# Sums of gate/up weights by accumulating DMAs, and another order of the seven block products

## The chip, the cores and the metric

The kernel runs on one core of one Trainium2 chip. Its engines are TensorE (PE, with its weight loads as PEld), VectorE (DVE), ScalarE (ACT), GpSimd (POOL) and SyncE (SP), which here issues nearly all transfers. The metric is the time of one execution on the device in microseconds (us), the median of several runs. A profile is one further execution, recorded instruction by instruction.

## The reference, cut to what matters

One decoder layer on 512 tokens of width 1024. Three head groups (mLSTM, SSD, retention) are computed from one input projection; their outputs are concatenated into `mix`. The change lies in what comes after that:

```
x = x + mix @ w_out
h = rmsnorm(x, norm_ffn)                      # y * rsqrt(mean(y*y) + eps) * g
gate, up = jnp.split(h @ w_gate_up, 2, axis=-1)
x = x + (jax.nn.silu(gate) * up) @ w_down
return rmsnorm(x, norm_final)
```

FFN_HIDDEN is 2816. All inputs are float32, and the products keep about that accuracy: each float32 operand is split into a high and a low part (`hi`, `lo`), and a product is three matmuls, hi*hi, hi*lo and lo*hi.

## The kernel before, in words

**Weights.** All weight matrices are packed into one array and cut into chunks, 256 rows by up to 512 columns, held as 128 x 1024 (512 KB). For each chunk `split` (lines 198 to 204) issues a cast on ACT, which makes `hi` (L202), and a subtraction on DVE, which makes `lo` (L203). There are four `hi` and four `lo` buffers. `chunk` (L225) fetches three chunks ahead of the one that the matmuls are about to use.

**Output projection.** `products_f` (L377) multiplies in two passes; the last pass covers two groups of four tiles of 128 features. Where a tile is done, `ev_out` adds it to `x` on DVE (L1125), scales it with the gain of the norm on ACT (L1129, into `y2`), feeds it to the norm and stores it to DRAM (`x2d`, L1131). `Norm.feed` squares a tile (on ACT for even k, L300, on POOL for odd k, L298) and adds the squares in a tree on DVE (L304). `finish` (L307) sums over the features with four tiny matmuls (L310); the result `r2` is needed only where gate and up are scaled.

**Gate and up.** Tokens are cut in two halves, features in two halves, and the columns in six pairs of blocks (five of 512 columns, one of 256: `GU_W`), one block of gate and one of up. In each pair the 2 x 2 block product is done with seven products instead of eight, in the manner of Strassen and Winograd. A product has 24 matmuls (L1164 to L1166) from two chunks. Four quarters of weights come in from DRAM per pair: R11, R12, R22, R21. Four products need sums of quarters: `tb` = R12 + R22, `r12` = R12 + R11, then `r11` = `tb` + R11 and `r21` = `r11` + R21. POOL forms all of them (L911, and L935 and L936 for the next pair), two instructions per sum. Their places in memory are rotated from pair to pair (`nxt`), and a place is loaded anew by SP as soon as its contents are split (`follow`). The other operand, sums of token and feature halves (names S1 to S4), is formed once, by DVE and POOL (L1118), and split by `split_a` (L1112 on ACT, L1113 on DVE). The order of the products is 11, S2, S1, S3, 12, S4, 22; 11 needs only the first half of the features. After each product its result is moved out of the PSUM banks by ACT and DVE (L1195 to L1225).

**Turning.** The results of a pair are transposed on PE in four groups of four (L1176), all 16 of them between the second and the third product of the next pair; the first four tiles go to DRAM (`ad`).

**Down projection.** At the start the residual `x2d` is read back (L1234) and added with transposing matmuls (L1264), then come the products (L1267 to L1269).

**Order of the work.** Each engine runs its instructions in order, and so does SP with its transfers. A scheduler in the framework sets this order when the kernel is built, from the order of the code and its own estimate of durations. Waits are semaphores that an instruction carries.

Of the kernel before, what the change touches and what calls it, by code (L numbers as in the profile page):

```python
# [16 lines left out]
P = 128  # L17
D = 1024
S = 512
NC = 4  # L20
# [99 lines left out]
def trunk(tc, x, xt, wcat, vecs, rows, consts, posn, gfin, out):  # L120
# [6 lines left out]
    with contextlib.ExitStack() as es:  # L127
# [160 lines left out]
        class Norm:  # L288
# [602 lines left out]
        def begin_ffn():  # L891
# [6 lines left out]
            def gload(p, quarter, to):  # L898
                if p < len(GU_W):
                    for s_ in range(2):  # L900
                        bring(GU0 + 8 * p + 2 * quarter + s_, to[s_])

            def pair_jobs(p, U):
                w2 = 2 * GU_W[p]
                nxt = dict(r11=U["spare"], r12=U["r12"], r22=U["tb"], tb=U["r11"], r21=U["r22"], spare=U["r21"])

                def of(r, s_):
# [5 lines left out]
                def sums(s_):  # L913
                    add("tb", "r12", "r22", s_)
                    add("r12", "r12", "r11", s_)

                order = []

                def job(role, s_, before=None, after=None):
                    def run():  # L920
                        if before:
                            before()
# [15 lines left out]
                def tc_():  # L938
                    for i in range(2):
                        add("r11", "tb", "r11", i)  # L940

                def td():
                    for i in range(2):
                        add("r21", "r11", "r21", i)
                    follow(U["r11"])

                def follow(unit, quarter=None, to=None):
# [9 lines left out]
                job("r11", 0, before=(lambda: sums(0)) if p == 0 else None)  # L957

                def after_p1():
                    if p == 0:  # L960
                        sums(1)
                    tc_()
                    if p:
                        follow(U["spare"], R11)

                job("r11", 1, after=after_p1)
                job("r11", 0)
                job("r11", 1)
                job("r12", 0)
                job("r12", 1, after=lambda: follow(U["r12"], R12))  # L970
                job("tb", 0)
                job("tb", 1, after=lambda: follow(U["tb"], R22))
                job("r21", 0)
                job("r21", 1, after=td)
                job("r22", 0)
                job("r22", 1, after=lambda: follow(U["r22"], R21))
                job("r21", 0, after=next_sums)
                job("r21", 1, after=lambda: follow(U["r21"]))
                return order, nxt
# [15 lines left out]
            for q, r in ((R11, "r11"), (R12, "r12"), (R22, "r22")):  # L995
                gload(0, q, roles[r])
# [123 lines left out]
        for last in (False, True):  # L1120
            for gr in range(2):

                def ev_out(t, ps):
                    d = x2[4 * gr + t]
                    dve.tensor_tensor(out=d, in0=ps, in1=d, op=ALU.add)  # L1125
                    if last:
                        k = 4 * gr + t
                        g = vec[:, V_G2 + k:V_G2 + k + 1]
                        act.activation(out=v3(y2[k // 2], 2)[:, k % 2, :], in_=d, func=AF.Copy, scale=g)  # L1129
                        n2.feed(d, t % 2 == 1)  # L1130
# [14 lines left out]
        s3 = [combine(pool, halves(i, 0), halves(i, 1), ALU.subtract) for i in range(2)]  # L1145
        s1 = [combine(dve, halves(i, 1), halves(2 + i, 1), ALU.subtract) for i in range(2)]
        s2 = [combine(dve, s1[i], halves(i, 0), ALU.subtract) for i in range(2)]
        s4 = [combine(pool, halves(2 + i, 0), s2[i], ALU.add) for i in range(2)]
        for name, src in (("S2", s2), ("S1", s1), ("S3", s3), ("12", [halves(2 + i, 0) for i in range(2)]), ("S4", s4), ("22", [halves(2 + i, 1) for i in range(2)])):
            for i in range(2):  # L1150
                split_a(name, i, src[i])
# [17 lines left out]
        def turn(p, w, a):  # L1169


            def go():
                for f in range(w // P):
                    ps = mbank()
                    for c in range(NC):
                        mm(ps[:, c * P:(c + 1) * P], lhsT=a[c][:, f * P:(f + 1) * P], rhs=ident, start=True, stop=True, is_transpose=True)  # L1176
                    kt = 4 * p + f
                    t = slot()
                    act.copy(out=t, in_=ps)
                    if kt < SPILL:  # L1180
                        sp.dma_start(out=ad[kt], in_=t)
                    else:
                        aT[kt] = t
# [3 lines left out]
        def cols(t, w):  # L1187
            return t[:, 0:w]

        for p, w in enumerate(GU_W):  # L1190
            ba = [bank() for _ in range(2)]
            product(ba, "11", w, True)
            s1 = [slot(w=w) for _ in range(2)]
            for c in range(2):
                act.copy(out=s1[c], in_=ba[c][:, 0:w])  # L1195
            if p == 0:
                n2.finish(r2)
            bb = [bank() for _ in range(2)]
            product(bb, "S2", w, True)
            e = [slot(w=w) for _ in range(2)]  # L1200
            for c in range(2):
# [3 lines left out]
            bq = [mbank() for _ in range(2)]  # L1205
            product(bq, "S1", w, True)
            product(bb, "S3", w, False)
# [3 lines left out]
            for c in range(2):  # L1211
                dve.tensor_tensor(out=u[c], in0=bq[c][:, 0:w], in1=u[c], op=ALU.subtract)
            product(ba, "12", w, False)
            g1 = [slot(w=w) for _ in range(2)]
            for c in range(2):
                act.activation(out=g1[c], in_=ba[c][:, 0:w], func=AF.Silu, scale=r2[:, c:c + 1])
            product(bq, "S4", w, False)
# [8 lines left out]
            tail.append(turn(p, w, e + u))  # L1226


        gf = [slot() for _ in range(2)]
        for hf in range(2):  # L1230
            sp.dma_start(out=gf[hf], in_=gfin[512 * hf:512 * hf + 512].partition_broadcast(P))
        for k in range(KD):
            x2[k] = slot()
            sp.dma_start(out=x2[k], in_=x2d[k])  # L1234
# [17 lines left out]
        for n, kc in enumerate(DOWN_ORDER):  # L1252
            w2 = [chunk(), chunk()]
            split_t(n + 2)
            for c in range(NC):
                if n == 0 and c == 2:
                    tail.pop(0)()
# [99 lines left out]
```

## Time and profile before

| | us |
|---|---|
| median of 3 runs (lowest, highest) | 861.02 (860.77, 861.97) |
| the profiled execution | 862.31 |
| its span | 860.5 |
| PE busy | 833.4 (97%) |
| DVE, ACT, POOL busy | 549.5, 375.0, 342.0 |
| bytes moved | 93.41 MB, 109 GB/s over the span |

The span is the time from the first to the last recorded instruction; the profiled execution is 1.8 us longer than it. PE is busy almost throughout, so the question for any change is in which stretches PE stands still or runs at its lower clock, and what it waits for there.

### The profile page before, as it was taken

What the parts mean: (1) busy time and instruction counts of PE and PEld (TensorE: products, weight loads), DVE (VectorE), ACT (ScalarE), POOL (GpSimd) and SP (SyncE); (2) the same over time, 40 slices, a digit from 0 to 9 for tenths busy, and PEclk for the clock granted to TensorE, in tenths of its full rate; (3) what the DMA queues carried; (4) which work ended last, traced back from release to release, by engine and by line L of the source; (5) the groups of instructions that cost most, each with busy time, mean ns of one, the idle gap of its engine ahead of it and who ended that gap; (6) DMA issues with size and microseconds to landing.
All of it is one profiled execution on the core that took longest, in us unless ns stands there. A gap on an engine that the chain in (4) does not pass through costs nothing. (4 is left out here: it accounts for less than half of the span.)

```text
span 860.5 us, 11249 instructions
## 1 busy us (share of the span) xinstructions
PE 833.4 (97%) x4238; PEld 715.4 (83%) x4238; DVE 549.5 (64%) x742; ACT 375.0 (44%) x641; POOL 342.0 (40%) x278
## 2 busy tenths in 40 slices
PE   9999999999999899999999889999999997999997
PEld 9989899898988788888888768787877887888885
DVE  6648677685648978366433989797979787122223
ACT  6344545364534354335312654545353556511113
POOL 2335433242024847613304638283838333920001
PEclk9999999999999999999999979999999999999999
DMA  7423332432234223216321253422232138530002
GB/s 249 153 75 106 98 122 81 126 95 68 98 99 146 71 93 109 74 50 254 138 98 50 98 196 98 146 98 98 99 98 74 50 116 317 204 98 0 1 1 98
DMA packets 32933, 93.41 MB, mean 109 GB/s; under 512 B 3800, under 2 KB 3928, under 8 KB 32880
## 3 DMA queue, kind: packets, MB, share of 16 engines
q1 hardware_dynamic: 32160, 91.58, 32.2%
q10 hardware_dynamic: 720, 1.12, 0.4%
q8 instruction: 33, 0.54, 0.3%
q14 instruction: 20, 0.16, 0.1%
HBM read 87.40 MB, written 5.29 MB: 108 GB/s over the span
## 5 line engine op out<-in xcount | busy, mean ns | idle before, releaser
L203 DVE TENSOR_TENSOR lo<-raw,hi 128x1024 fp32r<-128x1024 f32 (+3 forms) x98 | 131.5, 1346 | 132.9 <-ACT hi L202 132.3
L202 ACT CAST hi<-raw 128x1024 fp32r<-128x1024 f32 (+3 forms) x107 | 104.2, 976 | 161.5 <-PE b L388 79.7
L203 DVE TENSOR_TENSOR lo<-big,hi 128x1024 fp32r<-128x1024 f32 (+1 forms) x79 | 118.2, 1505 | 79.0 <-ACT hi L202 78.3
L202 ACT CAST hi<-big 128x1024 fp32r<-128x1024 f32 (+1 forms) x79 | 77.5, 991 | 135.0 <-PE m L1269 60.6
L387 PE MATMUL b<-s,hi 128*128 128x512 f32 x304 | 120.0, 395 | 0.8 <-ACT s L637 0.8
L388 PE MATMUL b<-s,hi 128*128 128x512 f32 x304 | 119.1, 392 | 0.0
L389 PE MATMUL b<-s,lo 128*128 128x512 f32 x304 | 118.5, 391 | 0.0
L370 PE MATMUL b<-hi,s 128*128 128x384 f32 (+2 forms) x320 | 114.7, 365 | 1.3 <-ACT big L408 1.0
L371 PE MATMUL b<-lo,s 128*128 128x384 f32 (+2 forms) x320 | 115.3, 360 | 0.0
L372 PE MATMUL b<-hi,s 128*128 128x384 f32 (+2 forms) x320 | 113.9, 361 | 0.0
L1165 PE MATMUL b<-lo,s 128*128 128x512 f32 (+1 forms) x240 | 90.3, 377 | 2.6 <-DVE lo L203 2.6
L1164 PE MATMUL b<-hi,s 128*128 128x512 f32 (+1 forms) x240 | 88.7, 376 | 4.0 <-ACT s L1112 3.2
L1166 PE MATMUL b<-hi,s 128*128 128x512 f32 (+1 forms) x240 | 89.7, 376 | 0.0
L387 PEld LDWEIGHTS b<-s,hi 128*128 128x128 f32 x304 | 57.1, 188 | 12.2 <-ACT s L637 1.1
L389 PEld LDWEIGHTS b<-s,lo 128*128 128x128 f32 x304 | 57.1, 188 | 11.5
L388 PEld LDWEIGHTS b<-s,hi 128*128 128x128 f32 x304 | 57.2, 188 | 10.9
L370 PEld LDWEIGHTS b<-hi,s 128*128 128x128 f32 x320 | 60.1, 188 | 6.5 <-ACT big L408 1.2
L371 PEld LDWEIGHTS b<-lo,s 128*128 128x128 f32 x320 | 60.2, 188 | 5.2 <-DVE lo L203 0.4
L372 PEld LDWEIGHTS b<-hi,s 128*128 128x128 f32 x320 | 60.0, 188 | 4.9
L203 POOL TENSOR_TENSOR lo<-raw,hi 128x1024 fp32r<-128x1024 f32 (+1 forms) x9 | 19.5, 2165 | 100.9 <-ACT hi L202 91.3
L618 DVE SCALAR_TENSOR_TENSOR s<-s,vec,s 128x511 f32<-128x511 f32 (+2 forms) x66 | 59.1, 939 | 0.2 <-ACT s L615 0.2
L1164 PEld LDWEIGHTS b<-hi,s 128*128 128x128 f32 x240 | 45.4, 190 | 13.2 <-ACT s L1112 3.6
(296 smaller groups left out, 1612.1 us busy)
## 6 DMA issues: line engine op xcount, KB each, us to landing
raw<-in_wcat SPq DMA_DIRECT2D x67, 512.0 KB, 3.4
big<-in_wcat SPq DMA_DIRECT2D x47, 512.0 KB, 4.5
raw<-in_wcat SPq DMA_DIRECT2D x20, 384.0 KB, 3.1
s<-in_xt SPq DMA_DIRECT2D x16, 256.0 KB, 6.3
s<-mdr SPq DMA_DIRECT2D x12, 256.0 KB, 4.4
s<-adr SPq DMA_DIRECT2D x12, 256.0 KB, 5.9
x2d<-s SPq DMA_DIRECT2D x8, 256.0 KB, 2.0
s<-x2d SPq DMA_DIRECT2D x8, 256.0 KB, 6.8
```

Of the source, the lines that this page charges most:

```text
L202: pin(act.copy(out=hi, in_=raw), first)
L203: pin(eng.tensor_tensor(out=lo, in0=raw, in1=hi.bitcast(F32), op=ALU.subtract), first)
L370: mm(o_, lhsT=hh, rhs=whi[:, k, :], start=kk == 0, stop=False)
L371: mm(o_, lhsT=hh, rhs=wlo[:, k, :], start=False, stop=False)
L372: mm(o_, lhsT=hl, rhs=whi[:, k, :], start=False, stop=kk == KD - 1)
L387: mm(banks[t], lhsT=wh, rhs=rhs_hi[kk], start=a, stop=False)
L388: mm(banks[t], lhsT=wh, rhs=rhs_lo[kk], start=False, stop=False)
L389: mm(banks[t], lhsT=wl, rhs=rhs_hi[kk], start=False, stop=b)
L618: dve.scalar_tensor_tensor(out=a[:, sft:S], in0=u[:, 0:S - sft], scalar=w[3 - sft], in1=a[:, sft:S], op0=ALU.mult, op1=ALU.add)
L1164: mm(o_, lhsT=ah, rhs=whi[:, k, :], start=first and s_ == 0 and k == 0, stop=False, skip_group_check=not first)
L1165: mm(o_, lhsT=ah, rhs=wlo[:, k, :], start=False, stop=False, skip_group_check=not first)
L1166: mm(o_, lhsT=al, rhs=whi[:, k, :], start=False, stop=s_ == 1 and k == 1, skip_group_check=not first)
```

## The change

Four things change in gate/up.

1. Of the four sums of weights in a pair, two are formed by transfers that add to what lies in their destination: `add_chunk` issues them on POOL's queue (`accum_op=ALU.add`). R12 is added onto a place loaded with R22 (`tb`), R11 onto a place loaded with R12 (`r12`). So R11, R12 and R22 are read twice: 14 chunks per pair instead of 8. The other two sums go to DVE (`onto`). POOL adds no weights any more.
2. The products come as 11, S3, S1, S2, 12, S4, 22. S3 needs only the first half of the features, as 11 does, and its operand is now formed and split during the output projection. S3 is copied out by ACT, and S2 accumulates on S3 in the same banks.
3. The squares of the norm overwrite `x` in place (after it is stored), their sums move from DVE to POOL, and the tiny matmuls of `finish` come after S2 in the code (before: after 11).
4. The 16 transposes of a pair are spread over four places, and `x2d` and the final gain are read back during the last pair instead of after it.

```diff
+        def add_chunk(i, t):
+
+            w = len(CHUNKS[i][2])
+            pool.dma_start(
+                out=t[:, 0:2 * w],
+                in_=wcat[offsets[i]:offsets[i] + P * 2 * w].rearrange("(p f) -> p f", p=P),
+                accum_op=ALU.add,
+            )
...
-            def feed(self, x_, on_pool):
+            def feed(self, x_, on_pool, adds=dve, own=True):
                 k, sq = len(self.sq), self.sq
-                sq.append(slot())
+                sq.append(slot() if own else x_)
...
-                    dve.tensor_tensor(out=sq[i], in0=sq[i], in1=sq[j], op=ALU.add)
+                    adds.tensor_tensor(out=sq[i], in0=sq[i], in1=sq[j], op=ALU.add)
...
-                def add(to, x_, y_, s_):
-                    pool.tensor_tensor(out=of(to, s_), in0=of(x_, s_), in1=of(y_, s_), op=ALU.add)
...
+                def onto(to, x_, s_):
+                    dve.tensor_tensor(out=of(to, s_), in0=of(x_, s_), in1=of(to, s_), op=ALU.add)
...
-                def next_sums():
-                    if p + 1 < len(GU_W):
-                        w_ = 2 * GU_W[p + 1]
-                        for i in range(2):
-                            t, a_, b_, c_ = (nxt[r][i][:, 0:w_] for r in ("tb", "r12", "r22", "r11"))
-                            pool.tensor_tensor(out=t, in0=a_, in1=b_, op=ALU.add)
-                            pool.tensor_tensor(out=a_, in0=a_, in1=c_, op=ALU.add)
...
+                def after_11():
+                    if p:
+                        onto("r11", "tb", 1)
+                        follow(U["spare"], R11)
+
+                def after_tb():
+                    if p == 0:
+                        for i in range(2):
+                            onto("r11", "tb", i)
+                    follow(U["tb"], R22)
+
+                def after_21():
+                    for i in range(2):
+                        onto("r21", "r11", i)
+                    follow(U["r11"], R22)
+
+                def after_22():
+                    follow(U["r22"], R21)
+                    gload(p + 1, R12, nxt["tb"], add=True)
...
+                job("r11", 0, (lambda: onto("r11", "tb", 0)) if p else None)
+                job("r11", 1, after_11)
+                job("tb", 0)
+                job("tb", 1, after_tb)
+                job("r12", 0)
+                job("r12", 1, after_12)
                 job("r11", 0)
-                job("r11", 1)
...
+                job("r11", 1, lambda: gload(p + 1, R11, nxt["r12"], add=True))
...
+                            split_a("S3", k // 2, combine(pool, halves(k // 2, 0), halves(k // 2, 1), ALU.subtract))
...
+        for k in range(KD):
+            n2.feed(x2[k], k % 2 == 1, adds=pool, own=False)
...
             bb = [bank() for _ in range(2)]
-            product(bb, "S2", w, True)
+            product(bb, "S3", w, True)
             e = [slot(w=w) for _ in range(2)]
             for c in range(2):
-                dve.tensor_tensor(out=e[c], in0=bb[c][:, 0:w], in1=s1[c], op=ALU.add)
-            if tail:
-                tail.pop(0)()
+                act.copy(out=e[c], in_=bb[c][:, 0:w])
+            turn_one()
+            if last:
+                for k in range(KD):
+                    x2[k] = slot()
+                    sp.dma_start(out=x2[k], in_=x2d[k])
             bq = [mbank() for _ in range(2)]
             product(bq, "S1", w, True)
-            product(bb, "S3", w, False)
+            turn_one()
+            product(bb, "S2", w, False)
+            if p == 0:
+                n2.finish(r2)
```

Three places show how the instructions move. The number behind a tile's name tells tiles of one name apart.

First DVE, where the last tiles of the output projection (L1125 before, L1129 after) meet the first products. `lo` are the low parts of weights, L304 the sums of the norm, L1118 (after: L1122) the sums S1 and S2. Before:

```order
L1125 TENSOR_TENSOR s_3853<-b_4397,s_3853 128x512
L304 TENSOR_TENSOR s_4442<-s_4442,s_4453 128x512
L1118 TENSOR_TENSOR s_4487<-big_4289 128x512
L203 TENSOR_TENSOR lo_4554<-big_4290,hi_4553 128x1024
L304 TENSOR_TENSOR s_4465<-s_4465,s_4476 128x512
L1118 TENSOR_TENSOR s_4489<-big_4289,big_4290 128x512
L1118 TENSOR_TENSOR s_4491<-s_4487,big_4289 128x512
L304 TENSOR_TENSOR s_4442<-s_4442,s_4465 128x512
L1118 TENSOR_TENSOR s_4493<-s_4489,big_4289 128x512
```

The same place after the change, with L1117 as the low parts of S1 and S2:

```order
L1129 TENSOR_TENSOR s_3853<-b_4402,s_3853 128x512
L212 TENSOR_TENSOR lo_4546<-raw_4294,hi_4545 128x1024
L1122 TENSOR_TENSOR s_4474<-big_4289,big_4290 128x512
L1117 TENSOR_TENSOR s_4477<-s_4472,s_4476 128x512
L1117 TENSOR_TENSOR s_4481<-s_4474,s_4480 128x512
L1122 TENSOR_TENSOR s_4484<-s_4472,big_4289 128x512
L1122 TENSOR_TENSOR s_4486<-s_4474,big_4289 128x512
L212 TENSOR_TENSOR lo_4566<-big_4291,hi_4565 128x1024
L212 TENSOR_TENSOR lo_4588<-big_4291,hi_4587 128x1024
L1117 TENSOR_TENSOR s_4489<-s_4484,s_4488 128x512
```

The sums of the norm are gone from DVE, and S1 is split before S2 is formed.

Next POOL from the squares of the norm (L298) on. Before, with L1118 as S3 and S4, L276 and L256 as `r2`, and L911 as sums of weights:

```order
L298 TENSOR_TENSOR s_4453<-s_3849 128x512
L298 TENSOR_TENSOR s_4476<-s_3853 128x512
L1118 TENSOR_TENSOR s_4483<-big_4289 128x512
L1118 TENSOR_TENSOR s_4485<-big_4289 128x512
L1118 TENSOR_TENSOR s_4495<-big_4289,s_4491 128x512
L1118 TENSOR_TENSOR s_4497<-big_4290,s_4493 128x512
L276 TENSOR_SCALAR r_841_4482<-ss_4594 128x4
L256 TENSOR_TENSOR r_841_4482<-r_841_4482,mhalf_106 128x4
L911 TENSOR_TENSOR big_4289<-big_4290,big_4289 128x1024 x2
```

After, with L307 as squares, L313 as sums of the norm, L1122 as S4, and L194 as the adding transfers:

```order
L307 TENSOR_TENSOR s_3849<-s_3849 128x512
L313 TENSOR_TENSOR s_3847<-s_3847,s_3849 128x512
L307 TENSOR_TENSOR s_3853<-s_3853 128x512
L313 TENSOR_TENSOR s_3851<-s_3851,s_3853 128x512
L313 TENSOR_TENSOR s_3847<-s_3847,s_3851 128x512
L313 TENSOR_TENSOR s_3839<-s_3839,s_3847 128x512
L1122 TENSOR_TENSOR s_4504<-big_4289,s_4484 128x512
L1122 TENSOR_TENSOR s_4506<-big_4290,s_4486 128x512
L194 DMA big_4291<-in_wcat 128x1024 x2
L285 TENSOR_SCALAR r_839_4471<-ss_4702 128x4
```

POOL has eight instructions from the square of the sixth tile to S4, and then the transfers and the few columns of `r2`.

Last SP at the end of the last pair, where `s<-x2d` is the reload of the residual (L1234, after: L1219) and L185 are weights. Before:

```order
L1231 DMA s_6348<-in_gfin 128x512
L1234 DMA s_6351<-x2d 128x512
L185 DMA big_4289<-in_wcat 128x1024
L1234 DMA s_6353<-x2d 128x512
L1234 DMA s_6355<-x2d 128x512
L1234 DMA s_6357<-x2d 128x512
```

After:

```order
L185 DMA raw_4294<-in_wcat 128x1024
L185 DMA big_4291<-in_wcat 128x1024 x2
L1219 DMA s_6147<-x2d 128x512
L1219 DMA s_6149<-x2d 128x512
L1219 DMA s_6151<-x2d 128x512
L1219 DMA s_6153<-x2d 128x512
```

The eight reloads now stand together, behind six chunks of the down projection and ahead of the final gain.

## Rows read from the trace of the kernel before

**Rows 1.** Page, part 1: busy time, share of the span, instructions.

```profile
PE 833.4 (97%) x4238; PEld 715.4 (83%) x4238; DVE 549.5 (64%) x742; ACT 375.0 (44%) x641; POOL 342.0 (40%) x278
```

**Rows 2.** Waits of PE, whole span: us in total, times, longest.

```profile
PE b L1264 <- DMA s<-x2d: 4.3, 2, 2.8
PE m L310 <- DVE s L304: 3.3, 1, 3.3
PE b L1164 <- ACT s L1112: 3.2, 1, 3.2
PE b L1165 <- DVE lo L203: 2.6, 4, 0.8
```

**Rows 3.** Windows: us, PE, PEld, DVE, ACT, POOL busy, PE's clock, DMA share, GB/s.

```profile
490.00:507.00 17.00, 10.51 (x35) 8.19 (x34) 17.00 (x19) 8.17 (x14) 8.84 (x6) 0.71 0.39 124
...
619.00:660.00 41.00, 40.18 (x184) 32.99 (x183) 35.10 (x29) 20.05 (x24) 23.91 (x9) 1.00 0.29 91
...
699.00:722.00 23.00, 23.00 (x183) 22.46 (x182) 16.14 (x27) 13.29 (x24) 4.28 (x3) 1.00 0.56 185
722.00:740.00 18.00, 13.67 (x78) 11.66 (x78) 7.28 (x9) 14.74 (x26) 12.53 (x10) 0.91 1.01 377
```

**Rows 4.** Timeline of PE, start of gate/up: start us, us, instruction.

```profile
486.81 0.39 PE L1164 MATMUL b<-hi,s 128*128 128x512 f32 x1
...
492.03 0.39 PE L1166 MATMUL b<-hi,s 128*128 128x512 f32 x1
...
503.24 0.63 PE L1165 MATMUL m<-lo,s 128*128 128x512 f32 x1
503.67 0.63 PE L1166 MATMUL b<-hi,s 128*128 128x512 f32 x1
```

**Rows 5.** Timeline of PE, later: two turns, last pair's start and end, down projection.

```profile
590.26 1.91 PE L1176 MATMUL m<-kst,s 128*128 128x128 f32 x16
...
631.46 1.91 PE L1176 MATMUL m<-kst,s 128*128 128x128 f32 x16
...
701.98 0.28 PE L1164 MATMUL b<-hi,s 128*128 128x256 f32 x1
...
723.74 0.28 PE L1166 MATMUL b<-hi,s 128*128 128x256 f32 x1
...
732.79 0.39 PE L1268 MATMUL b<-lo,s 128*128 128x512 f32 x1
```

**Rows 6.** Timeline of DVE: last tiles of the output projection, and one low part.

```profile
485.71 1.99 DVE L1125 TENSOR_TENSOR s<-b,s 128x512 f32<-128x512 f32 x3
...
576.04 1.21 DVE L203 TENSOR_TENSOR lo<-big,hi 128x1024 fp32r<-128x1024 f32 x1
```

**Rows 7.** Groups of DVE, 540 to 690: busy us, mean ns, idle before.

```profile
L203 DVE TENSOR_TENSOR lo<-big,hi 128x1024 fp32r<-128x1024 f32 x37 | 60.1, 1635 | 13.1 <-ACT hi L202 13.0
```

**Rows 8.** Groups of POOL: 459 to 474 (DVE nearly idle), then 505 to 690.

```profile
L911 POOL TENSOR_TENSOR raw<-big 128x1024 f32<-128x1024 f32 x1 | 2.4, 2402 | 46.5 <-DVE lo L203 46.5
...
L935 POOL TENSOR_TENSOR big<-big,big 128x1024 f32<-128x1024 f32 x5 | 16.6, 3310 | 0.2
```

**Rows 9.** Norm: POOL's timeline, one square; DVE's sums (L304), duration min/median/max.

```profile
486.47 1.04 POOL L298 TENSOR_TENSOR s<-s 128x512 f32<-128x512 f32 x1 [3.57 <-DVE s L1125]
...
L304 DVE TENSOR_TENSOR s<-s,s x7: 676/684/2293, 480.0 to 498.2; 128x512 f32<-128x512 f32 x7
```

**Rows 10.** DMA issues: count, KB each, median us from issue to landing.

```profile
big<-in_wcat SPq DMA_DIRECT2D x47, 512.0 KB, 4.5
...
x2d<-s SPq DMA_DIRECT2D x8, 256.0 KB, 2.0
s<-x2d SPq DMA_DIRECT2D x8, 256.0 KB, 6.8
```

**Rows 11.** Groups of ACT, 540 to 690: copies out of PSUM.

```profile
L1195 ACT COPY s<-b 128x512 f32<-128x512 f32 x8 | 4.2, 581 | 0.0
```

**Rows 12.** Timeline of SP's queue: issues of the reload.

```profile
721.61 4.73 SPq L1234 DMA_DIRECT2D s<-x2d  x5
...
727.30 1.59 SPq L1234 DMA_DIRECT2D s<-x2d  x2
```

More of the change, by code (lines that the diff above doesn't have):

```diff
@@ L896, in begin_ffn, with gload @@
             roles = dict(r11=b2[1:3], r12=b3[0:2], r22=[b3[2], rw[0]], tb=rw[1:3], r21=b1[0:2], spare=[b1[2], b2[0]])
[L898 removed]
+            def gload(p, quarter, to, add=False):
                 if p < len(GU_W):
                     for s_ in range(2):
[L901 removed]
+                        (add_chunk if add else bring)(GU0 + 8 * p + 2 * quarter + s_, to[s_])
             def pair_jobs(p, U):
@@ L905, in pair_jobs, with job @@
                 nxt = dict(r11=U["spare"], r12=U["r12"], r22=U["tb"], tb=U["r11"], r21=U["r22"], spare=U["r21"])
+                order = []
                 def of(r, s_):
                     return U[r][s_][:, 0:w2]
-                def add(to, x_, y_, s_):
-                    pool.tensor_tensor(out=of(to, s_), in0=of(x_, s_), in1=of(y_, s_), op=ALU.add)
[L913 to L919, printed above, removed]
+                def onto(to, x_, s_):
+                    dve.tensor_tensor(out=of(to, s_), in0=of(x_, s_), in1=of(to, s_), op=ALU.add)
+                def job(role, s_, after=None):
                     def run():
-                        if before:
-                            before()
                         r_ = split(of(role, s_), dve)
@@ L928, in job, with follow @@
                     order.append(run)
-                def next_sums():
-                    if p + 1 < len(GU_W):
-                        w_ = 2 * GU_W[p + 1]
-                        for i in range(2):
-                            t, a_, b_, c_ = (nxt[r][i][:, 0:w_] for r in ("tb", "r12", "r22", "r11"))
-                            pool.tensor_tensor(out=t, in0=a_, in1=b_, op=ALU.add)
-                            pool.tensor_tensor(out=a_, in0=a_, in1=c_, op=ALU.add)
[L938 to L947, printed above, removed]
+                def follow(unit, quarter=None):
                     if p + 1 < len(GU_W):
@@ L994, in begin_ffn @@
             jobs.extend(down_job(j) for j in range(len(CHUNKS) - DN0))
-            for q, r in ((R11, "r11"), (R12, "r12"), (R22, "r22")):
-                gload(0, q, roles[r])
+            gload(0, R11, roles["r11"])
+            gload(0, R22, roles["tb"])
+            gload(0, R12, roles["r12"])
+            gload(0, R22, roles["r22"])
+            gload(0, R12, roles["tb"], add=True)
+            gload(0, R11, roles["r12"], add=True)
             return lambda: (gload(0, R21, roles["r21"]), gload(1, R11, roles["spare"]))
@@ L1167, in product, with turn, turn_one @@
                 tick()
-        def turn(p, w, a):
+        def turn(p, f, a):
             def go():
[L1173 to L1183, printed above, removed]
-            return go
-        def cols(t, w):
-            return t[:, 0:w]
+                ps = mbank()
+                for c in range(NC):
+                    mm(ps[:, c * P:(c + 1) * P], lhsT=a[c][:, f * P:(f + 1) * P], rhs=ident, start=True, stop=True, is_transpose=True)
+                kt = 4 * p + f
+                t = slot()
+                act.copy(out=t, in_=ps)
+                if kt < SPILL:
+                    sp.dma_start(out=ad[kt], in_=t)
+                else:
+                    aT[kt] = t
+            return go
+        def turn_one():
+            if tail:
+                tail.pop(0)()
+        gf = [None] * 2
         for p, w in enumerate(GU_W):
+            last = p == len(GU_W) - 1
             ba = [bank() for _ in range(2)]
@@ L1210, in trunk @@
                 dve.tensor_tensor(out=u[c], in0=bb[c][:, 0:w], in1=s1[c], op=ALU.add)
-            for c in range(2):
+                dve.tensor_tensor(out=e[c], in0=u[c], in1=e[c], op=ALU.subtract)
                 dve.tensor_tensor(out=u[c], in0=bq[c][:, 0:w], in1=u[c], op=ALU.subtract)
+            turn_one()
+            if last:
+                for hf in range(2):
+                    gf[hf] = slot()
+                    sp.dma_start(out=gf[hf], in_=gfin[512 * hf:512 * hf + 512].partition_broadcast(P))
             product(ba, "12", w, False)
@@ L1225, in trunk @@
                 dve.scalar_tensor_tensor(out=u[c], in0=u[c], scalar=r2[:, 2 + c:3 + c], in1=s1[c], op0=ALU.mult, op1=ALU.mult)
[L1226 to L1234, printed above, removed]
+            tail.extend(turn(p, f, e + u) for f in range(w // P))
         for k in range(SPILL):
@@ L1256, in trunk @@
                 if n == 0 and c == 2:
-                    tail.pop(0)()
+                    while tail:
+                        turn_one()
                     banks += [mbank() for _ in range(4)]
```

47 lines of the change are left out of this document (22 added, 25 removed).

## The prediction

> **What bounds the kernel now.** I read the page's busy times first: PE is busy for 97% of the span [rows 1], so only stretches where PE waits or runs at its lower clock can be won. PE's waits come next: the long ones all lie in gate/up and behind it, 4.3 us for the reloaded residual, 3.3 for the norm's sums, 3.2 for the split of S2, 2.6 in four pieces for low parts of weights [rows 2]. The windows place them: from 490 to 507 PE is busy for 10.5 of 17 us at a mean granted clock of 0.71, part of it at 1.2 GHz instead of 2.4; from 722 to 740 for 13.7 of 18 us at 0.91; elsewhere nearly full at 1.00 [rows 3].
>
> The timeline gives the whole loss. The first product of gate/up has 24 matmuls, the first starting at 486.81, the last at 492.03, so one takes 5.22 / 23 = 0.227 us [rows 4]. A pair is 7 x 24 = 168 of them, 38.1 us, and its 16 transposes take 1.9 [rows 5]. From 486.81 to the first matmul of the half-wide last pair, 701.98, five pairs and four sets of transposes would take 5 x 38.1 + 4 x 1.9 = 198.1 us. They take 215.2: 17.1 us are lost [rows 4, 5]. Two turns of later pairs stand 41.2 us apart (590.26 and 631.46) where 40.0 would do: 1.2 lost per pair, 4.9 over four. The other 12.2 fall to the first pair: 6.5 us of waits [rows 2], and matmuls 0.43 us apart after them [rows 4], the clock having fallen behind two waits close together. At the start of the down projection the lost time is 4.3 us of waits plus about half of the 3.3 us that PE then needs to be back at full spacing at 732.79, 5.9 us in all [rows 2, 5]. To be won: 12.2 + 4.9 + 5.9 = 23.0 us.
>
> **The change part by part.**
>
> *Start of gate/up (12.2 us).* S3 takes S2's place behind product 11, and its operand needs nothing of the last four tiles. S1 now comes as the third product, 10.9 us after 486.81, at 497.7; S2 as the fourth. S1's split is done a few DVE instructions after the last tile (added by 487.7 [rows 6]): the 3.2 us wait goes. The norm's matmuls stand behind S1 in PE's order, so its sums may be 11 us later than before: the 3.3 us wait goes too. With both gone nothing lowers the clock.
>
> What is late next is DVE, slowed by POOL. The rows show that the two hold each other up: a low part takes 1.21 us by itself [rows 6] and 1.64 on average beside POOL's sums [rows 7]; a POOL sum 2.40 us with DVE nearly idle and 3.31 beside it [rows 8]; a sum of squares on DVE, mostly 0.68, once 2.29 [rows 9]. The norm on POOL makes this worse for a while. From the last tile (487.7, and 0.5 for the rest of its path) to the low part of the second half of S2's weights DVE has 16 instructions, by the order of the changed kernel: five 1024-wide low parts at 1.21 and eleven 512-wide sums and low parts at 0.66 (1.99 / 3) [rows 6], 13.3 us in all. POOL has eight instructions in the same time, 4 sums, 2 squares, 2 for S4, at 1.04 [rows 9], 8.3 us. One after the other: 488.2 + 21.6 = 509.8. PE needs that low part after 3.5 products, 486.81 + 19.0 = 505.8. So PE waits some 4 us in there; S2's start also hangs on ACT's casts of S4, behind the same POOL chain. I take 5.5 us, and 1.5 for smaller waits like those of the other pairs: gain 12.2 - 7.0 = 5.2. If the two engines did not disturb each other DVE would be done at 501.5 and nothing would wait: gain 12. If the waits are 9 or more and the clock falls again: gain 0.
>
> The Trainium skill ("SBUF — State Buffer", section "SBUF: two separate sides") states that DVE and GpSimd share a port pair which one of them holds for a whole instruction while the other is blocked. The trace agrees as far as 2.40 against 3.31 goes [rows 8]. By that rule the two sums add up fully and the term is the 5.2 taken; if they only shared bandwidth it would lie between 5.2 and 12.
>
> *Pairs one to four (4.9 us).* POOL's sums go, eight per pair at up to 3.3 us. DVE takes two sums over, four instructions at 1.21 = 4.8 us per pair, and loses the hold-ups: 14 low parts x (1.64 - 1.21) = 6.0 [rows 6, 7]. It is busy for 35.1 of 41.0 us now [rows 3], about 34 after. ACT gets two copies of 0.58 [rows 11] and is busy for half of the time. I take a gain of 4; bounds 0 and 4.9.
>
> *The adding transfers.* The trace has none. The nearest row is a plain load of the same 512 KB, landed after 4.5 us [rows 10]. I take 6 for one, and this hides: R22's place is free at about 16 and 20 us into a pair (low parts of R21 and their sums done); loaded 4.5 later; the adding transfer then lands at about 27 and 31. By the order DVE asks for the first half only behind the evacuation of S4, at 33, and PE does not stand still before 38 to 40. So 11 us of cover for the first, more for the second half. Bytes: 14 chunks instead of 8, with two thirds of a pair's engines' time free at a DMA share of 0.29 [rows 3]. Below nothing it cannot be, since no work of PE goes. The upper end is the third rival. On POOL the two first issues stand between the last gatings of the retention heads; cost 0, since an issue computes nothing, bound 2 by two sums of 1.04 [rows 9] in their place.
>
> The Trainium skill ("Collectives: The Full Stack", section "The bandwidth ceiling: the fold count and why AG ≠ RS ≠ AR") says that a transfer with an add reads two sources and so runs at half of a copy's rate. No run here shows it yet. By it, as an estimate from that page, four adds and ten loads weigh like 18 chunks, well within a pair.
>
> *Last pair.* DVE gets four sums of 0.68 = 2.7 us, in 23 us of which it is busy for 16.1 [rows 3]. Cost 0, bound 1.5.
>
> *Start of the down projection (5.9 us).* The reloads were issued from 721.6 to past 727.3 [rows 12] and took 6.8 to land [rows 10], with DMA at a share of 1.01 [rows 3]. Now they wait only for places that products 11 and S3 of the last pair free, about 5 us into it, some 707. Six chunks of weights stand ahead of them in SP's queue: 3 MB and 2 MB of residual at 377 GB/s [rows 3] take 13 us, so they are there by about 720, before PE asks at 724. Gain 5.5; if they come 3 to 4 us late after all, 2.
>
> Sum: 5.2 + 4 + 5.5 - 0.2 for the small bounds = 14.5 us off the profiled execution's 862.3, 847.8. The median of the runs is 1.3 us under that execution: **846.5 us**.
>
> **The rivals.**
>
> *All waits go.* DVE keeps up in the first pair and the clock stays: 12 + 4.9 + 5.9 = 22.8 off, 838.2 on the runs. For it: POOL's sums leave the whole stretch. Against it: DVE is full from 490 to 507 [rows 3] and half of what held it up, POOL, gets more to do there.
>
> *The wait moves.* S1 or S2 is late by more than 6 us and the clock falls as before, or the reload stands in SP's queue behind weights whose places come free late. The first gives 862.3 - 4 - 5.5 - 1.3 = 851.5, the second 846.5 + 3.5 = 850, both 855.
>
> *Slower: the adding transfer is slow.* Four of them per pair go through one queue, so from 10 us each they set the pair's 40 us, whatever the cover. At 12 us each a pair takes 48: sums for five later pairs, the last half as large, cost 4.5 x 8 = 36, less some 9 of the gains that stay: 888. For it: nothing in the trace shows such a transfer, and POOL's sequencer has to make it while DVE is busy for 85% of a pair. Against it: 512 KB at 377 GB/s is 1.4 us of all queues, so it would have to be eight times slower than a copy.
>
> *The change doesn't do what it says*: the order shows the S3 operand, the norm and the reloads where the diff puts them, so only nothing gained anywhere would do it, 861.
>
> **How the numbers follow.** Forecast 40%, all waits gone 15%, the wait moves 26%, slow transfers 13%, nothing gained 3%, another loss over 863 3%. The likeliest case's own range is 843 to 850. The range to hold 8 in 10 leaves out the slow transfers and a little at the lower end: 839 to 858. What a measurement of this kernel can tell from no change is about 0.2%, 1.7 us, so faster means under 859.3 and slower over 862.7: faster 80%, same 4%, slower 16%.
>
> **What would show it right or wrong.** Right: no wait of PE for the norm or for the residual; turns or first products of later pairs 40.0 to 40.3 us apart; waits of 4 to 7 us in all around 497 to 510, on low parts or ACT's casts, with POOL's sums of squares beside them; the adding transfers landing in under 10 us. Wrong: pairs further apart than 41.2 us with DVE or ACT waiting for transfers of POOL's queue; the residual waited for again; a granted clock under 1.00 in the middle of gate/up.

## The result, and the profile after

The changed kernel takes 847.2 us (4 runs, 846.03 to 848.6) against 861.5 for the one before beside it: ratio 0.9833, 95% interval 0.9812 to 0.9853. Its profiled run took 848.60 us, span 846.8, 13.7 less than the profiled run before.

PE first: the page's busy time, then its longest waits (us in total, times, longest), to be held against [rows 1] and [rows 2].

```profile
PE 829.4 (98%) x4238; PEld 713.6 (84%) x4238; DVE 536.2 (63%) x759; ACT 382.6 (45%) x653; POOL 253.0 (30%) x261
```

```profile
PE m L1177 <- DVE lo L212: 3.6, 1, 3.6
...
PE m L1187 <- DVE s L1249: 1.3, 2, 1.0
```

The waits for the residual, the norm's sums and the split of S2 are gone. One of 3.6 us for a low part of weights is new, and one of 1.3 for the last turn. The windows of the same stages as in [rows 3] (columns as there; the last two shifted to where the last pair now ends):

```profile
490.00:507.00 17.00, 13.41 (x50) 10.57 (x49) 16.91 (x13) 11.47 (x18) 14.18 (x9) 0.81 0.68 203
619.00:660.00 41.00, 41.00 (x190) 33.77 (x189) 30.17 (x34) 22.24 (x27) 3.45 (x4) 1.00 0.64 157
691.00:714.00 23.00, 23.00 (x188) 22.69 (x188) 16.84 (x30) 14.88 (x27) 1.00 (x1) 1.00 0.86 310
714.00:732.00 18.00, 16.71 (x96) 13.70 (x95) 10.63 (x8) 11.06 (x20) 14.67 (x11) 1.00 0.57 219
```

In the second and third window PE is full; DVE is down from 35.1 to 30.2 us of 41 in the second; the granted clock is below full in the first alone. PE's timeline (start us, us, instruction) of the start, two turns and the ends, against [rows 4, 5]:

```profile
486.94 0.39 PE L1176 MATMUL b<-hi,s 128*128 128x512 f32 x1
...
497.82 0.61 PE L1176 MATMUL m<-hi,s 128*128 128x512 f32 x2
502.02 0.80 PE L1177 MATMUL m<-lo,s 128*128 128x512 f32 x1 [3.58 <-DVE lo L212]
502.62 0.63 PE L1178 MATMUL m<-hi,s 128*128 128x512 f32 x1
...
507.28 0.39 PE L1178 MATMUL m<-hi,s 128*128 128x512 f32 x1
...
509.55 0.95 PE L319 MATMUL m<-ones,s 128*128 128x1 f32 x8
...
629.40 0.60 PE L1187 MATMUL m<-kst,s 128*128 128x128 f32 x4
...
669.46 0.60 PE L1187 MATMUL m<-kst,s 128*128 128x128 f32 x4
...
692.64 0.28 PE L1176 MATMUL b<-hi,s 128*128 128x256 f32 x1
...
840.32 0.39 PE L1288 MATMUL m<-hi,s 128*128 128x512 f32 x1
```

and PE's last matmul before the change:

```profile
854.32 0.39 PE L1269 MATMUL m<-hi,s 128*128 128x512 f32 x1
```

Two lengths can be read from these, and for every run below. A, from the first product of gate/up to the first half-wide matmul: 215.2 us before, 692.64 - 486.94 = 205.7 after; the prediction's sum for products and transposes alone is 198.1. B, from there to PE's last matmul: 854.32 - 701.98 = 152.3 before, 147.7 after. A gave 9.5 us, B 4.7; what lies ahead and behind took back 0.4.

### The profile page after: what moved, and what is told of

It reads as the page before. It is cut to its first block, busy times and chain, and to the rows that moved or that the text cites. A ratio compares the mean times of both kernels' runs of the same rounds, so it can differ in the third digit from the quotient of the medians.

```text
span 846.8 us, 11293 instructions
## 1 busy us (share of the span) xinstructions
PE 829.4 (98%) x4238; PEld 713.6 (84%) x4238; DVE 536.2 (63%) x759; ACT 382.6 (45%) x653; POOL 253.0 (30%) x261
## 3 DMA queue, kind: packets, MB, share of 16 engines
q1 hardware_dynamic: 33888, 97.35, 34.3%
q0 software_dynamic: 3456, 11.54, 7.8%
## 4 chain that ended last, share of the span: by engine, by line
PE 58%; DVE 6%; POOL 3%; DMA 2%; issue 2%; ACT 1%; SPq 0%; POOLq 0%; ACTq 0%; DVEq 0%
PE b L1176 6%; PE b L1178 6%; PE b L1177 6%; PE b L397 4%; PE b L398 4%; PE b L396 4%; PE m L1177 3%; PE m L1178 2%; PE m L1176 2%; PE m L1287 2%; PE m L1288 2%; PE m L1286 2%; PE b L1286 2%; PE b L1287 2%; PE b L1288 2%
## 5 line engine op out<-in xcount | busy, mean ns | idle before, releaser
L212 DVE TENSOR_TENSOR lo<-raw,hi 128x1024 fp32r<-128x1024 f32 (+3 forms) x98 | 118.7, 1215 | 118.7 <-ACT hi L211 118.2
L212 DVE TENSOR_TENSOR lo<-big,hi 128x1024 fp32r<-128x1024 f32 (+1 forms) x79 | 96.8, 1227 | 88.7 <-ACT hi L211 88.1
L398 PEld LDWEIGHTS b<-s,lo 128*128 128x128 f32 x304 | 57.4, 189 | 11.7
L194 POOL DMA_DIRECT2D big<-in_wcat x19 | 16.8, 884 | 137.3 <-DMA big<-in_wcat 127.3
```

The source lines that it names most:

```text
L212: pin(eng.tensor_tensor(out=lo, in0=raw, in1=hi.bitcast(F32), op=ALU.subtract), first)
L398: mm(banks[t], lhsT=wl, rhs=rhs_hi[kk], start=False, stop=b)
```

## The experiments

All are edits of the changed kernel. Ratios are against the kernel before in the same session (861.5 to 862.0); A and B come from PE's timeline.

| run | median us | ratio (95%) | A | B |
|---|---|---|---|---|
| the change | 847.2 | 0.9812 to 0.9853 | 205.7 | 147.7 |
| e1 adds left out | 846.1 | 0.9804 to 0.9837 | 204.8 | 147.7 |
| e2 reload late | 853.4 | 0.9884 to 0.9919 | 205.3 | 153.8 |
| e3 sums on POOL | 876.5 | 1.0153 to 1.0187 | 233.7 | 147.7 |
| e4 sums on DVE | 861.3 | 0.9980 to 1.0003 | 218.8 | 147.7 |
| e5 norm cut | 841.1 | 0.9744 to 0.9772 | 199.6 | 147.7 |
| e6 norm's sums on DVE | 845.0 | 0.9789 to 0.9817 | 203.6 | 147.7 |
| e7 old order | 851.1 | 0.9864 to 0.9892 | 209.6 | 146.8 |
| e8 turns together | 845.8 | 0.9799 to 0.9826 | 205.4 | 146.6 |
| e9 norm's sums on PE | 845.5 | 0.9790 to 0.9819 | 203.1 | 147.7 |
| e10 sums on DVE, apart | 847.6 | 0.9818 to 0.9847 | 206.1 | 147.7 |
| e11 adds twice | 858.9 | 0.9951 to 0.9979 | 216.4 | 147.7 |
| e12 late sums | 842.3 | 0.9763 to 0.9791 | 201.5 | 146.6 |

### What the adding transfers cost (e1, e11)

```diff
 def add_chunk(i, t):
-    w = len(CHUNKS[i][2])
-    pool.dma_start(...)
+    return
```

> The changed kernel (847.2 us) with the adding transfers left out: tb and r12 then hold R22 and R12 alone, so their products are of other numbers, but every matmul, split and sum stays. Theory: the adding transfers (median 7.9 us from issue to landing in the changed kernel's profile) are hidden whole, since PE shows no wait for anything that hangs on them: 846 to 848, turns of later pairs 40.0 to 40.1 us apart as now. Rival: they slow the plain loads or POOL's and DVE's work, so the kernel without them is faster by 2 us or more, most of it before the middle of the first pair, where four chunks are being added and the DMA share is 0.88.

846.1 us, A 0.9 shorter: hidden but for some 1 us at most. What one takes is on the page of the changed kernel (KB each, median us from issue to landing; then queues: packets, MB, share of 16 engines' span):

```profile
big<-in_wcat SPq DMA_DIRECT2D x54, 512.0 KB, 4.4
big<-in_wcat POOLq DMA_DIRECT2D x17, 512.0 KB, 7.9
...
q1 hardware_dynamic: 33888, 97.35, 34.3%
q0 software_dynamic: 3456, 11.54, 7.8%
```

```diff
-    (add_chunk if add else bring)(...)
+    for _ in range(2 if add and p > 1 else 1):
+        (add_chunk if add else bring)(...)
```

> The changed kernel with every adding transfer of pairs 2 to 5 issued twice, the second into the same place behind the first (so R12 and R11 are added twice there, and the products are of other numbers). A place is then ready about 8 us later than now, and the queue carries eight instead of four per pair. Theory (the cover of some 11 us that the prediction took): no wait of PE in pairs, 846 to 848.5, pairs 40.0 to 40.3 apart. Rival (the slow transfer of the prediction): the cover is under 8 us, or eight transfers slow the plain loads: pairs 41 to 48 apart, 851 or more.

858.9 us, in the rival's range: the cover is not without end. DVE now waits three times for a transfer at the start of a pair, 7.8, 6.5 and 5.7 us, and PE for a low part behind each, 3.3, 2.0 and 1.1 (waits of DVE and of PE, then PE's timeline at the start of the third pair):

```profile
DVE big L922 <- DMA big<-in_wcat: 14.4, 2, 7.8
DVE raw L922 <- DMA big<-in_wcat: 5.7, 1, 5.7
PE b L1178 <- DVE lo L212: 6.5, 3, 3.3
```

```profile
575.67 0.27 PE L1188 MATMUL m<-kst,s 128*128 128x128 f32 x1
579.26 0.77 PE L1178 MATMUL b<-lo,s 128*128 128x512 f32 x1 [3.32 <-DVE lo L212]
```

The dose was larger than the expectation said: POOL waits for the first transfer of a half before it issues the second, and the other half's stand behind it, so the last issue ahead of the third pair comes at 572.94, where the changed kernel has it at 558.88. The waits also tell what PE can bear. DVE's is longer than PE's by 4.5 us each time (7.8 - 3.3, 6.5 - 2.0, 5.7 - 1.1): by so much the sum can be late before PE stands still.

### The reload (e2)

```diff
-            if last:
-                for k in range(KD):
-                    x2[k] = slot()
-                    sp.dma_start(out=x2[k], in_=x2d[k])
 ...  # behind the last pair
+        for k in range(KD):
+            x2[k] = slot()
+            sp.dma_start(out=x2[k], in_=x2d[k])
```

> The changed kernel with the eight reloads of the residual issued after the last pair's products again, and nothing else moved in the code. Theory (the prediction's step on the start of the down projection): PE waits for the residual again, 4.3 us of waits and about 1.6 of low clock as before the change, less the 1.3 us that PE now waits there for the last turn: 847.2 + 4.6 = 851.8. Rival: with POOL out of the pairs and the products in the new order the reload is early enough anyway, or PE does the last turn meanwhile: 847 to 848.

853.4 us: A as it was, B 6.1 longer. PE's waits:

```profile
PE b L1282 <- DMA s<-x2d: 5.8, 1, 5.8
```

The theory holds, and its 4.6 was small against 6.2.

### Who adds the weights, and where in the order (e3, e4, e10)

```diff
 def after_22():
     follow(U["r22"], R21)
-    gload(p + 1, R12, nxt["tb"], add=True)
+    for i in range(2):   # t, a_, c_ = tb, r12, r11 of pair p + 1
+        pool.tensor_tensor(out=t, in0=t, in1=a_, op=ALU.add)   # e4: dve
+        pool.tensor_tensor(out=a_, in0=a_, in1=c_, op=ALU.add) # e4: dve
 ...
-job("r11", 1, lambda: gload(p + 1, R11, nxt["r12"], add=True))
+job("r11", 1)
```

> The changed kernel with tb and r12 of pairs 1 to 5 formed by POOL again (two instructions per sum, both after the sixth product's weights are split), not by adding transfers; pair 0 keeps the transfers. Theory: DVE and POOL hold each other up; DVE's low parts, 1.22 us now, go back to a mean of about 1.6 while a POOL sum runs, and pairs are 40.6 to 41.2 us apart: half of what POOL did before, so +2 to +4.5, 849 to 852. Rival: only the total of DVE's work counts and there is room for it (30.0 of 40 us busy): pairs stay at 40.1 and the time at 847 to 848.

> The changed kernel with tb and r12 of pairs 1 to 5 formed by DVE at the same places as in the run with POOL's sums; pair 0 keeps the adding transfers. DVE gets four more instructions of 1.22 us per pair: 30.0 + 4.9 = 34.9 of 40 us, as busy as before the change (35.1 of 41), but alone. Theory (what cost the old kernel its 1.2 us per pair was two engines holding each other up, not DVE's load): pairs stay 40.0 to 40.2 apart, 847 to 848, and the adding transfers would then not have been needed from the second pair on. Rival: at 35 of 40 us DVE is late with low parts whoever else runs: pairs 40.6 to 41.2, 849 to 852.

Both fell outside either expectation: 876.5 and 861.3. The groups of DVE from 540 to 690 (busy us, mean ns, idle before), first beside POOL's sums:

```profile
L212 DVE TENSOR_TENSOR lo<-big,hi 128x1024 fp32r<-128x1024 f32 x33 | 49.8, 1512 | 13.5 <-ACT hi L211 13.5
L1234 DVE TENSOR_TENSOR s<-s,s 128x512 f32<-128x512 f32 x6 | 13.5, 2288 | 0.0
...
L1233 DVE TENSOR_TENSOR s<-b,s 128x512 f32<-128x512 f32 x6 | 3.8, 678 | 0.0
```

then with the same sums on DVE and POOL idle:

```profile
L212 DVE TENSOR_TENSOR lo<-big,hi 128x1024 fp32r<-128x1024 f32 x34 | 41.5, 1219 | 16.0 <-ACT hi L211 16.0
...
L1233 DVE TENSOR_TENSOR s<-b,s 128x512 f32<-128x512 f32 x8 | 5.4, 681 | 0.0
L1234 DVE TENSOR_TENSOR s<-s,s 128x512 f32<-128x512 f32 x8 | 5.4, 681 | 0.0
```

The hold-up between the two engines is real. In e3 POOL's four sums stand in a bunch, from 605.8 to 617.1, and the timeline shows which of DVE's instructions they hold up (POOL's line first, then two of DVE's beside it). PE's longest waits of that run are for an evacuation further down DVE's list (last line).

```profile
608.29 3.26 POOL L965 TENSOR_TENSOR big<-big 128x1024 f32<-128x1024 f32 x1
609.22 1.27 DVE L1233 TENSOR_TENSOR s<-b,s 128x512 f32<-128x512 f32 x2
610.41 4.49 DVE L1234 TENSOR_TENSOR s<-s,s 128x512 f32<-128x512 f32 x2
```

```profile
PE m L1181 <- DVE s L1235: 13.2, 3, 5.1
```

But in e4, with POOL idle, pairs still stood 43.9 us apart. DVE's timeline of one pair shows why: all four sums (L964, L965; one of them ahead of these rows, at 596.58) stand among the evacuations ahead of the low part that PE waits for.

```profile
599.45 1.22 DVE L965 TENSOR_TENSOR big<-big 128x1024 f32<-128x1024 f32 x1
600.59 0.68 DVE L1233 TENSOR_TENSOR s<-b,s 128x512 f32<-128x512 f32 x1
601.19 1.21 DVE L964 TENSOR_TENSOR big<-big,big 128x1024 f32<-128x1024 f32 x1
...
604.66 1.22 DVE L965 TENSOR_TENSOR big<-big,raw 128x1024 f32<-128x1024 f32 x1
605.79 1.22 DVE L212 TENSOR_TENSOR lo<-raw,hi 128x1024 fp32r<-128x1024 f32 x1
```

```profile
604.44 0.70 PE L1181 MATMUL b<-hi,s 128*128 128x512 f32 x2
607.06 0.50 PE L1182 MATMUL b<-lo,s 128*128 128x512 f32 x1 [1.92 <-DVE lo L212]
```

Load or place? e10 keeps e4's sums and sets them apart:

```diff
+def next_sum(to, x_, s_):     # kept in program order on DVE
+    pin(dve.tensor_tensor(out=t, in0=t, in1=a_, op=ALU.add))
 after_22():            next_sum("tb", "r12", 0)
 job("r21", 0, lambda:  next_sum("tb", "r12", 1))
 job("r21", 1, ...      next_sum("r12", "r11", 0))
 job("r11", 0, ...      onto("r12", "r11", 1))   # next pair
```

> The run with the sums of tb and r12 on DVE gave 861.3 where 847 to 848 or 849 to 852 was expected. Its pairs are 43.9 us apart though DVE is busy for only 34.8 of 44: the four sums stand together between the low parts of product 12 and of S4, and PE waits 1.9 us for S4's and runs slowly behind it. Here the same four sums per pair stand apart in DVE's order, each kept behind another low part, the last behind the first low part of the next pair; no adding transfers from pair 1 on. Theory (what decides is what stands ahead of a low part, not DVE's load): pairs 40.0 to 40.3 apart, 846 to 849. Rival (the load decides, 35 of 40): pairs 42 to 44, 855 to 861.

847.6 us, pairs 40.1 apart (turns at 634.04 and 674.16). The window 525 to 690 (columns as above) has PE full:

```profile
525.00:690.00 165.00, 165.00 (x758) 135.52 (x757) 143.31 (x155) 86.82 (x107) 0.00 (x0) 1.00 0.38 123
```

DVE is busy for 143.3 of 165 us there, 34.7 of 40. In these pairs place decides, not load, and the adding transfers were not needed from the second pair on: sums on DVE in the right places do the same.

### The start of gate/up (e5, e6, e7, e9)

```diff
 for k in range(KD):
-    n2.feed(x2[k], k % 2 == 1, adds=pool, own=False)
+    if k < 4:                                             # e5
+        n2.feed(x2[k], k % 2 == 1, adds=pool, own=False)  # e6: every k, adds=dve
```

> The changed kernel without the squares and sums of the norm for the last four tiles of the output projection (left out, so r2 is of the first four tiles alone); POOL then has two squares, three sums and S3, S4 there. DVE's own list and order stay. In the changed kernel PE waits 3.6 us at 498 for the low part of r12 and runs 13 matmuls at the lower clock behind it, 6.4 us in all. Theory: POOL's norm work holds DVE up (512-wide sums 1.3 to 1.8 us instead of 0.68, low parts 1.7 to 2.3 instead of 1.21), and without it the low part is there by about 498 to 499: 841 to 843. Rival: DVE's own list is too long there, with S2's sums ahead of that low part: the wait falls by under 1 us, 845 to 847.

841.1 us, as the theory has it. DVE's list from the last tile (L1129) to the two low parts of r12, and the last low part of S2's weights, in the changed kernel:

```profile
490.29 0.68 DVE L1129 TENSOR_TENSOR s<-b,s 128x512 f32<-128x512 f32 x1
...
496.30 3.46 DVE L1122 TENSOR_TENSOR s<-s,big 128x512 f32<-128x512 f32 x2
499.68 4.51 DVE L212 TENSOR_TENSOR lo<-big,hi 128x1024 fp32r<-128x1024 f32 x2
...
509.95 1.21 DVE L212 TENSOR_TENSOR lo<-big,hi 128x1024 fp32r<-128x1024 f32 x1
```

and in e5, up to the first low part of r12:

```profile
488.61 0.68 DVE L1129 TENSOR_TENSOR s<-b,s 128x512 f32<-128x512 f32 x1
...
492.31 1.29 DVE L1122 TENSOR_TENSOR s<-s,big 128x512 f32<-128x512 f32 x2
493.52 2.32 DVE L212 TENSOR_TENSOR lo<-big,hi 128x1024 fp32r<-128x1024 f32 x1
```

From the start of the last tile to the end of that low part DVE needs 7.2 us here. In the changed kernel PE got it at 502.0, 11.7 us after the last tile's start. What shrinks is mostly what stands ahead of it (the two sums 1.29 instead of 3.46). The low part itself stays slow, 2.32, beside POOL's sums for S4, which e5 keeps (493.17 to 496.99).

> The changed kernel with the norm's sums on DVE again (squares stay in place on POOL and ACT, the matmuls of the norm stay behind S2). By the order two of the seven sums then stand between the last tile and the low part of r12 that PE waits for, 2 x 0.68 = 1.4 us, and four sums, 1.04 us alone and up to 2.3 beside DVE, leave POOL in that stretch. Theory (hold-ups between the two add up): net 2 to 3 us earlier, the wait shrinks to 0.5 to 1.5 us, 843 to 845. Rival (DVE is the bound by itself): the wait grows by 1 us or more, 848 to 849.

845.0 us, at the upper end of the theory's range, and the wait 2.4, longer than it had. Moving the sums to POOL was the wrong way: on DVE they cost some 2 us less.

```diff
-product(bb, "S3", w, True)   # jobs r11, tb, r12, r11 + tb
+product(bb, "S2", w, True)   # jobs r11, r11 + tb, r12, tb
 ...
-product(bb, "S2", w, False)
+product(bb, "S3", w, False)
 ...  # and DVE moves S2 out, as before the change
```

> The changed kernel with the products in the old order again, 11, S2, S1, S3, 12, S4, 22, the weights split in that order, and DVE moving S2 out; the rest (transfers that add, norm on POOL with its matmuls behind the fourth product, spread turns, early reload) stays. Theory: the order is what takes the start's wait away; S1 and S2 are now asked for at 492.4 instead of 497.8, the low part of r12 is there at 502, so PE waits 8 to 9 us instead of 3.6 with the clock low after it: 852 to 854. Rival: PE's order (S1 before S2 is possible) and the freed norm sums absorb it: 847 to 849.

851.1 us, between the two. PE waits three times, 2.8 + 2.6 for casts of ACT and 1.2 for a low part, 6.6 us against 3.6, and A is 3.9 longer: the order is worth some 4 us at the start, less than the theory's 5 to 7. PE's order takes two matmuls of S1 ahead of S2 there, which may be why. B is 0.9 shorter: PE waits 0.6 us for the last turn, not 1.3.

```diff
-n2.feed(x2[k], k % 2 == 1, adds=pool, own=False)
+n2.feed(x2[k], k % 2 == 1 and k < 4, adds=pool if k < 4 else None, own=False)
 ...
-n2.finish(r2)
+n2.finish(r2, (0, 4, 5, 6, 7))   # tiny matmuls add five tiles
```

> The changed kernel with the norm taken off POOL without leaving anything out: the last four squares are formed on ACT (0.63 us each, ACT busy for about 11 of 17 us there), and are not added by any engine; PE's tiny matmuls of the norm add five tiles instead of one, 20 instead of 4. Leaving that work out altogether gave 841.1 us, so with 16 more tiny matmuls (five of them in 0.25 to 0.6 us in the changed kernel, so 1 to 2 us): theory 842 to 843.5, with no wait of PE at 498. Rival: four more squares on ACT delay the casts that DVE's low parts wait for, and a wait of 1 to 3 us stays: 844 to 846.

845.5 us, in the rival's range but not for its reason: the wait is gone, as the theory said, but 16 tiny matmuls cost 3.5 us (A against e5's), not 1 to 2. DVE's two low parts of r12 took 4.55 us here, as slow as in the changed kernel, yet in time, since the instructions ahead of them were done sooner. The timeline has each as two records, 22 in 2.4 us (502.38 to 504.75):

```profile
502.38 2.51 PE L320 MATMUL m<-ones,s 128*128 128x1 f32 x22
```

### The turns in one place (e8), and a faster version (e12)

```diff
 product(bq, "S1", w, True)
-turn_one()       # and at three other places
+while tail:
+    turn_one()
```

> The changed kernel with the transposes of a pair issued in one place of the code again (behind S1), not in four. Theory: spreading them bought nothing by itself; pairs 40.0 to 40.2 apart, 846.5 to 848. Rival: of the 1.2 us lost per pair before, the 0.5 that PE's waits for low parts do not explain came from the block: pairs 40.5 apart, 849.

845.8 us, a little under the theory's range: A 0.3 shorter, B 1.1. Spreading the transposes bought nothing in the pairs; it makes PE wait the 1.3 us for the last turn.

```diff
 product(bb, "S2", w, False)
+if p == 0:
+    for i, j in ((4, 5), (6, 7), (4, 6), (0, 4)):
+        pin(dve.tensor_tensor(out=sq[i], in0=sq[i], in1=sq[j], op=ALU.add))
 ...
 product(ba, "12", w, False)
+if p == 0:
+    n2.finish(r2)
```

with the last four squares on ACT as in e9 and the turns as in e8.

> A version made from the runs before: the last four squares of the norm on ACT, their four sums on DVE but behind the first low part of S4's weights (about 513), the tiny matmuls of the norm four again and behind product 12 in the code, and the transposes of a pair in one place. With the norm on PE the stretch from the first product to the half-wide pair took 203.1 us, of which 3.5 are the tiny matmuls (records of one, 0.11 us each, two per matmul); without the norm's last tiles 199.6. Theory: 200 to 202 us for it, up to 1.5 us of it a wait of PE for r2's way through ACT and POOL ahead of the second pair; the transposes in one place take 1 us off the end of the last pair as in that run: 841 to 843.5. Rival: the sums on DVE delay the low parts behind them (DVE is just in time there), PE waits 2 us or more and the clock falls: 845 to 848.

842.3 us, as the theory has it, ratio 0.9763 to 0.9791: faster than both kernels. PE's longest wait for a low part there:

```profile
PE m L1177 <- DVE lo L212: 0.7, 1, 0.7
```

## Why the prediction was right, step by step

*Start of gate/up* (taken 5.2 gained, 7.0 left). The 3.2 and 3.3 us waits went. Left are 7.3: A's 205.7 - 198.1 less 0.3 in later pairs. Of it the 15 matmuls from 497.82, the last starting at 507.28, took 9.7 us instead of 3.4: a wait of 3.6 and 2.7 of the lower clock behind it. Another 0.8 are the norm's four tiny matmuls (509.55, eight records), which the 198.1 leaves out. The mechanism was right, DVE held up by POOL's norm work (e5, e6; in e9 and e12 too the wait goes or shrinks to 0.7, though ACT forms the squares that e5 leaves out).

That the sizes agree, 7.0 and 7.3, is in part luck. The sum had 5.5 of wait, 1.5 of small waits and no low clock; the wait measured, 3.6, lies just under the 4 to 7 that were to show it right. The place was wrong as well: I looked at S2's second half, done at 509.8 by the sum (511.2 measured), wanted at 505.8. DVE's 16 instructions took 20.2 us, where the sum had 21.6 (13.3 undisturbed), but the last tile was added at 491.0, not at 487.7: two errors that nearly cancel. In the same list r12's first low part, three low parts of weights earlier, was wanted at 498.3 and there at 502.0, so PE stopped one product sooner and S2's was no longer late. "With both gone nothing lowers the clock" failed with it.

The Trainium skill ("SBUF — State Buffer", section "SBUF: two separate sides") names the DVE instructions that take the shared port pair: those in a two-port mode and, against a GpSimd instruction that reads SBUF, those with two SBUF inputs. The trace of e3 agrees, which the prediction had not weighed: beside POOL's sums DVE's sums of two SBUF tiles took 2.29 us, those with one operand from PSUM 0.68.

*Pairs one to four* (4 gained). 41.2 us apart became 669.46 - 629.40 = 40.06, 4.6 gained: the term was right. POOL does hold DVE up (e3 against e4). The other suspects that were tried are out: with the old order of the products (e7, turns 40.1 apart), the transposes in one place (e8, 40.0) or as much work on DVE as before the change (e10, 40.1) the gain stays. That the old kernel's 1.2 us hung on POOL's sums is shown in this way, by exclusion; no run puts them back at their old places. Two things the sum had wrong. DVE was to be busy for about 34 us of a pair, and 30.2 were measured: the 1.64 in the sum is the mean of the low parts from `big` places, and those from `raw` places, in the same window before the change, were held up more:

```profile
L203 DVE TENSOR_TENSOR lo<-raw,hi 128x1024 fp32r<-128x1024 f32 x15 | 31.3, 2092 | 6.9 <-ACT hi L202 6.9
```

And it weighed DVE's load, where the place of single instructions ahead of a low part decides (e4 against e10).

*The adding transfers* (6 us taken, hidden). They took 7.9 and were hidden but for 1 us at most (e1). That an issue costs POOL nothing is not so: each takes 0.86 us there. The cover came out nearly as said. In the changed kernel POOL issues a `tb` transfer at 595.28, and DVE sums from it at 608.95:

```profile
595.28 0.86 POOL L194 DMA_DIRECT2D big<-in_wcat  x1 [8.33 <-DMA big<-in_wcat]
```

```profile
608.95 1.22 DVE L921 TENSOR_TENSOR big<-big,big 128x1024 f32<-128x1024 f32 x1
```

With 7.9 us to land that is some 6 us to spare for DVE, and PE bears 4.5 more (e11): some 10 us in this pair, where the prediction had 6 and 5.

*Last pair and down projection* (5.5 gained, at no cost in the pair). B fell by 4.7. No wait for the residual, no low clock (e2 gives both back, 6.1 us, with a granted clock of 0.89 from 714 to 745). The missing 0.8 is the wait for the last turn, 1.3 us, which the prediction did not see: the spread of the transposes (e8).

*Sum.* 14.5 off the profiled run was said, 13.7 came; 846.5 for the median, 847.2 came. Of the rivals, the wait that moves is the one that came in part: it moved, but was 3.6 us, not over 6. That the waits at the start go needs the norm's last tiles off POOL (e5, e9, e12). The slow transfer did not come; e11 is what it would look like.

## What to carry to other kernels

Where an engine runs its list in order, work out for every entry that another engine waits for when it is done and when it is wanted, not only for the last; the first that is late stops the other engine, and takes the later ones' lateness away. Before work is moved to another engine or to a transfer, try it on the same engine at another place in the order: four sums per pair in a bunch cost 14 us here, the same four apart nothing (e4, e10). Moving small sums to an engine that shares something with the busy one can cost more than it frees (e6).

## What the runs showed of the hardware

- POOL holds up only part of DVE's work: in e3 a 512-wide sum of two SBUF tiles took 2.29 us, of PSUM and SBUF 0.68, while a POOL sum ran beside both.
- An adding transfer of 512 KB landed after 7.9 us (a plain one 4.4). Per MB its queue took 7.8 / 11.54 against 34.3 / 97.35 of the engines' time, 1.9 times as much (over all transfers of each queue, whatever their size). The Trainium skill ("Collectives: The Full Stack", section "The bandwidth ceiling: the fold count and why AG ≠ RS ≠ AR") has ReduceScatter at about half of AllGather's rate, because the add needs two source reads. It says so of collectives, and the prediction took it over to a kernel's own transfer; the 1.9 here agrees with that.
- A matmul of one float32 column takes 0.22 us on PE, in two records (e9, at the full clock); a 512-column one of the products, on split operands, takes 0.23.
